# A 1 MB pair transfer issued as two transfers of 512 KB, for even and odd SBUF partitions

## The chip, the cores and the metric

The kernel runs on one core of one Trainium2 chip. Times are microseconds (us) of device time of one execution, as medians of several runs; a profile is one profiled execution, and its span is some 2 us shorter than the run's time.

## The reference, cut to what matters

Each of 65,536 tokens has 1024 numbers, seen as 16 heads of 64. A routing product picks one head per token. That head's 64 numbers are multiplied by that head's 64x64 matrix; all other heads of the output are zero.

```python
# x: (64, 1024, 1024) float32; route_w: (1024, 16); experts: (16, 64, 64)
route_logits = x @ route_w
best_head = np.argmax(route_logits, axis=-1)
x_heads = x.reshape(B, S, H, Dh)
for h in range(H):
    mask = (best_head == h)
    transformed = np.matmul(x_heads[:, :, h, :], experts[h])
    out[:, :, h, :] = transformed * mask[:, :, None]
```

The kernel reads 268 MB and writes 268 MB.

## The kernel before

It works on pairs: 256 tokens, two for each of 128 SBUF partitions, so 8 KB per partition and 1 MB per pair. SyncE (SP) issues every load and store. TensorE (PE) transposes the tokens and multiplies them; the profile counts 108 matmuls for a pair. Five of eight blocks of 128 columns take the "split pass" with small 64x64 matmuls (80 of the 108), three take whole 128x128 blocks (12), and 16 are transposes. The calls of the split pass and of the whole blocks appear as two matmuls each. ScalarE (ACT), VectorE (DVE) and GpSimd (POOL) move results out of PSUM, where this kernel's matmuls put them (the `ps_` tiles), and mask them. SBUF is the memory that holds the tokens; its tiles here have 128 partitions.

```python
P = 128
XIN_BUFS = 10
OUT_BUFS = 6
AHEAD = 7                     # loads run seven pairs ahead
...
xg = x.rearrange("b s d -> (b s) d").rearrange("(g p t) d -> g p t d", p=P, t=2)
og = out.rearrange("b s d -> (b s) d").rearrange("(g p t) d -> g p t d", p=P, t=2)
...
def load(g):
    xin = xin_pool.tile([P, 2, D], FP32, name="xin", tag="xin")
    nc.sync.dma_start(out=xin, in_=xg[g])
    return xin
...
def split_pass(xt):
    ...                       # per token tile: 5 blocks x 4 matmuls of 64x64 on 80 columns
def whole_block(ps, xt, f):
    ...                       # one 128x128 matmul on 144 columns
...
for j in range(-2 * AHEAD, NT + 2, 2):
    if j + 2 * AHEAD < NT:
        xins[j + 2 * AHEAD] = load(j // 2 + AHEAD)
    if j < 0:
        continue
    pair = [i for i in (j - 2, j - 1) if i >= 0]
    for i in pair:
        work[i] = split_pass(xts[i])
    ...                       # transposes of pair j mixed with whole blocks of the pair before
                if i == pair[1]:
                    nc.sync.dma_start(out=og[i // 2], in_=ot)
```

SP works in program order: a store waits for its pair's result (869.7 us in 256 waits for DVE in before), and the next load stands behind it (issued 0.44 us after the store, median of the trace). The build gives DMA transfers eight completion semaphores in turn (both traces show eight for SP), and a transfer waits until the one eight places before it has landed: in after none is issued earlier, and the closest comes 16 ns later. So at most eight transfers of SP are in flight; the traces count at most seven in before.

Of the kernel before, what the change touches and what calls it, by code (L numbers as in the profile page):

```python
# [13 lines left out]
AX = mybir.AxisListType  # L14

P = 128
XIN_BUFS = 10
OUT_BUFS = 6
XT_BUFS = 5
# [5 lines left out]
def kernel(  # L25
# [19 lines left out]
    nc = tc.nc  # L45
# [3 lines left out]
    N = B * S  # L49
    NB = D // P  # L50
    NT = N // P
    HB = 512
# [4 lines left out]
    STEP = 2 * Dh + H  # L57
    assert D % P == 0 and N % P == 0 and Dh * H == D and 2 * Dh == P and NB == 8

    xg = x.rearrange("b s d -> (b s) d").rearrange("(g p t) d -> g p t d", p=P, t=2)  # L60
    og = out.rearrange("b s d -> (b s) d").rearrange("(g p t) d -> g p t d", p=P, t=2)

    consts = ctx.enter_context(tc.tile_pool(name="consts", bufs=1))
    small = ctx.enter_context(tc.tile_pool(name="small", bufs=4))
    xin_pool = ctx.enter_context(tc.tile_pool(name="xin", bufs=XIN_BUFS))
    xt_pool = ctx.enter_context(tc.tile_pool(name="xt", bufs=XT_BUFS))
# [5 lines left out]

    ident = consts.tile([P, P], FP32, name="ident")
    make_identity(nc, ident)
# [8 lines left out]
    with nc.allow_non_contiguous_dma(reason="constants, once"):  # L83
        for ab in range(2):
            e0, r0 = (0, Dh) if ab == 0 else (H, 0)
            for half in range(2):
                nc.scalar.dma_start(  # L87
                    out=mv[half * Dh:(half + 1) * Dh, ab::2, e0:e0 + Dh], in_=ev[half][:, ab:NS:2, :])
            nc.scalar.dma_start(out=mv[:, ab::2, r0:r0 + H], in_=rv[:, ab:NS:2, :])
        for half in range(2):  # L90
            nc.scalar.dma_start(
                out=mf[half * Dh:(half + 1) * Dh, :, H + half * Dh:H + (half + 1) * Dh],
                in_=ev[half][:, NS:, :])
# [7 lines left out]

    def load(g):
        xin = xin_pool.tile([P, 2, D], FP32, name="xin", tag="xin")
        nc.sync.dma_start(out=xin, in_=xg[g])
        return xin

    def transposes(xin, t, xt):

        for half in range(2):
            ps_t = ps_t_pool.tile([P, NB // 2, P], FP32, name="ps_t", tag="ps_t")  # L110
            for q in range(NB // 2):
                p = half * (NB // 2) + q
                nc.tensor.transpose(ps_t[:, q, :], xin[:, t, p * P:(p + 1) * P], ident)  # L113
                if q == NB // 2 - 1:
                    nc.scalar.copy(out=xt[:, half * (NB // 2):(half + 1) * (NB // 2), :], in_=ps_t)  # L115
                yield
# [10 lines left out]
    def split_pass(xt):  # L127
        ps = ps_s_pool.tile([P, 2, HB], FP32, name="ps_s", tag="ps_s")
        for p in range(NS):
            s, ab = divmod(p, 2)  # L130
            o0 = s * STEP + ab * Dh
            for half in range(2):
                for th in range(2):
                    nc.tensor.matmul(  # L134
                        ps[th * 64:(th + 1) * 64, half, o0:o0 + W],
                        lhsT=xt[half * 64:(half + 1) * 64, p, th * 64:(th + 1) * 64],
                        rhs=mv[half * 64:(half + 1) * 64, p, :],
                        start=(p == 0), stop=(p == NS - 1), skip_group_check=True)
        RW = (NS // 2) * STEP + Dh
        raw = raw_pool.tile([P, 2, SLOTS * STEP], FP32, name="raw", tag="raw")  # L140
        nc.scalar.copy(out=raw[:, :, 0:RW], in_=ps[:, :, 0:RW])  # L141
        lgs = small.tile([P, H], FP32, name="lgs", tag="lgs")
        logits(lgs, ps)
        return raw, lgs

    def whole_block(ps, xt, f):
        o0 = f * STEP + Dh
        nc.tensor.matmul(  # L148
            ps[:, o0:o0 + STEP], lhsT=xt[:, NS + f, :], rhs=mf[:, f, :],
            start=(f == 0), stop=(f == NF - 1), skip_group_check=True)  # L150

    def finish(ot, ps, raw, lgs):
        lgw = small.tile([P, H], FP32, name="lgw", tag="lgw")
        logits(lgw, ps)
        lg = small.tile([P, H], FP32, name="lg", tag="lg")
        nc.vector.tensor_add(out=lg, in0=lgs, in1=lgw)  # L156
        mx = small.tile([P, 8], FP32, name="mx", tag="mx")
        nc.vector.max(out=mx, in_=lg)  # L158
        ix = small.tile([P, 8], U32, name="ix", tag="ix")
        nc.vector.max_index(out=ix, in_max=mx, in_values=lg)  # L160
        mask = small.tile([P, H], FP32, name="mask", tag="mask")
        nc.vector.tensor_scalar(  # L162
            out=mask, in0=hid, scalar1=ix[:, 0:1], scalar2=None, op0=ALU.is_equal)

        ov = ot.rearrange("k (p two e) -> k p two e", two=2, e=Dh)
        mk = mask.rearrange("k (p two) -> k p two", two=2)

        def bc(m):
            return m.unsqueeze(3).to_broadcast(list(m.shape) + [Dh])

        nc.vector.tensor_tensor(  # L171
            out=ov[:, NS:], in1=bc(mk[:, NS:]), op=ALU.mult,
            in0=ps[:, W:W + NF * STEP].rearrange("k (f w) -> k f w", w=STEP)[:, :, 0:2 * Dh]
            .rearrange("k f (two e) -> k f two e", two=2))
        rv4 = raw.rearrange("k two (s w) -> k s two w", w=STEP)
        for ab in range(2):
            n = (NS + 1 - ab) // 2
            o0 = ab * W
            nc.gpsimd.tensor_tensor(  # L179
                out=ov[:, ab:NS:2], in0=rv4[:, 0:n, :, o0:o0 + Dh], in1=bc(mk[:, ab:NS:2]),  # L180
                op=ALU.mult)
# [7 lines left out]
# [8 lines that stand above are left out]
        tr = iter(())  # L197
        if j < NT:
            for i in (j, j + 1):
                xts[i] = xt_pool.tile([P, NB, P], FP32, name="xt", tag="xt")  # L200
            xin = xins.pop(j)
            tr = chain(transposes(xin, 0, xts[j]), transposes(xin, 1, xts[j + 1]))
        order = ORDER if pair else "T" * (2 * NB)
        f = 0
        for step in order:
            if step == "T":
                next(tr, None)
                continue
            i = pair[f // NF]
            if f % NF == 0:  # L210
                ps_w = ps_w_pool.tile([P, HB], FP32, name="ps_w", tag="ps_w")
            whole_block(ps_w, xts[i], f % NF)
            f += 1
            if f % NF == 0:
                if i == pair[0]:
                    ot = out_pool.tile([P, 2, D], FP32, name="ot", tag="ot")
                finish(ot[:, i % 2, :], ps_w, *work.pop(i))
                xts.pop(i)
                if i == pair[1]:
                    nc.sync.dma_start(out=og[i // 2], in_=ot)  # L220


# [28 lines left out]
```

## Time and profile before

| | before |
|---|---|
| time, median of 4 runs | 1370.2 us (1369.3 to 1372.3) |
| PE busy | 94% of the span |
| queue q1 (all loads and stores) | 97.6% of 16 engines' time |
| PE waits for "issue" in the split pass | 54.1 us |
| PE waits for a load | 6.5 us |

Lines of the page of before: the span; the busy time and share of the engines; the DMA queues (packets, MB, share of 16 engines' span); the chain of waits by engine; the issues of loads (count, KB each, median us from issue to landing; stores took 12.7 us).

```profile
span 1367.4 us, 65580 instructions
...
PE 1291.7 (94%) x27648; PEld 1210.8 (89%) x27648; DVE 928.0 (68%) x4098; ACT 924.1 (68%) x1537; POOL 721.9 (53%) x1031
...
q1 hardware_dynamic: 73728, 536.90, 97.6%
q8 instruction: 218, 3.57, 1.0%
...
PE 93%; issue 4%; DMA 2%; ACT 0%; DVE 0%; POOL 0%; ACTq 0%; POOLq 0%; DVEq 0%
...
xin<-in_x_dram SPq DMA_DIRECT2D x256, 1024.0 KB, 14.8
...
```

The wait list of PE in before (engine, line, what it waited for: us in total, times, longest in us):

```profile
...
PE ps_s L134 <- issue: 54.1, 71, 2.2
PE ps_t L113 <- DMA xin<-in_x_dram: 6.5, 2, 5.9
...
```

The wait list of SP in before:

```profile
...
SPq L220 <- DVE ot L171: 869.7, 256, 9.0
...
```

Three stretches of before (stretch, length, busy us and count of PE, PE weight loads, DVE, ACT, POOL, then PE clock, DMA share, GB/s):

```profile
...
100.00:300.00 200.00, 191.06 (x4090) 179.04 (x4086) 137.27 (x607) 136.56 (x228) 107.00 (x152) 1.00 1.01 403
300.00:500.00 200.00, 192.79 (x4154) 181.03 (x4144) 139.20 (x612) 138.74 (x231) 108.46 (x155) 1.00 1.01 404
1300.00:1367.40 67.40, 57.73 (x1268) 54.24 (x1260) 44.61 (x198) 41.36 (x69) 35.81 (x52) 0.96 0.73 299
...
```

How to read these. A packet is one piece that one DMA engine moves, here mostly 8 KB: q1 has 65,536 of them in before and 8192 of 4 bytes, 16 for each of the 512 transfers, at 9 ns each (median). The small ones are called completion packets below. PE leads the chain, and it hardly ever waits for data. Its own idle time is "issue", which means that no wait in the profile explains it. The trace does: each such stall ends about 1.4 us after one of the 218 packets of 16 KB on queue q8 has landed; there are 71 waits for 218 packets. q8 carries PE's instructions (27,648 matmuls and as many weight loads in 218 blocks are 254 a block), and PE's stalls stand a multiple of 256 of its instructions apart, give or take one, counted in the trace with the semaphore instructions (55,818 in all, 256 a block; 53 of 67 distances fit exactly, the others miss by one). A fetch takes an engine from q1: while a packet of q8 is in progress, 15.0 packets of q1 are, on average, and otherwise 16.0 (trace, 100 to 1300 us). At the same time the DMA share is 1.01: the engines are never idle in the middle (packet records overlap a little, so a full queue shows slightly over 1). Both resources look full.

The trace's packet records say: an 8 KB packet takes 309 ns in the median and 324.9 ns on average.

### The profile page before, as it was taken

Reading aid. Unit: us, or ns where it says so; the run is one execution under the profiler, and the core shown is the slowest. Engines: PE = TensorE matmul, PEld = TensorE weight load, DVE = VectorE, ACT = ScalarE, POOL = GpSimd, SP = SyncE. Lnnn points to the kernel's source line nnn. Section 1 sums busy time; section 2 is a strip of 40 time slices with the busy share of each in tenths; the row PEclk is TensorE's granted clock in tenths of the full one; section 3 lists DMA queues with packets and bytes.
Section 4 is the critical chain, followed back from the end, with each engine's and each line's share of the span. In section 5 each row is a group of like instructions: output and inputs, shape, how many; then the busy total and the mean of one; then the engine's idle time right before and its main releaser. Section 6 shows DMA issues by size and latency. Waiting matters only on the chain.

```text
span 1367.4 us, 65580 instructions
## 1 busy us (share of the span) xinstructions
PE 1291.7 (94%) x27648; PEld 1210.8 (89%) x27648; DVE 928.0 (68%) x4098; ACT 924.1 (68%) x1537; POOL 721.9 (53%) x1031
## 2 busy tenths in 40 slices
PE   7999999999999999999899999999999998999997
PEld 6899988899889999999899989998899998998996
DVE  3667666667666767667667766766667766766676
ACT  4676666677666667676666666766667666766675
POOL 2555555555555555555555555555555554555555
PEclk9999999999999999999999999999999999999999
DMA  9999999999999999999999999999999999999995
GB/s 348 421 418 407 408 394 400 402 401 409 409 400 397 402 414 411 404 405 402 395 399 397 402 393 406 401 405 393 382 399 409 410 407 388 395 415 393 397 381 220
DMA packets 76214, 541.43 MB, mean 396 GB/s; under 512 B 10384, under 2 KB 10384, under 8 KB 10384
## 3 DMA queue, kind: packets, MB, share of 16 engines
q1 hardware_dynamic: 73728, 536.90, 97.6%
q8 instruction: 218, 3.57, 1.0%
q10 hardware_dynamic: 2192, 0.33, 0.1%
q14 instruction: 76, 0.62, 0.1%
HBM read 268.76 MB, written 268.44 MB: 393 GB/s over the span
## 4 chain that ended last, share of the span: by engine, by line
PE 93%; issue 4%; DMA 2%; ACT 0%; DVE 0%; POOL 0%; ACTq 0%; POOLq 0%; DVEq 0%
PE ps_t L113 35%; PE ps_s L134 30%; PE ps_w L148 27%; DMA xin<-in_x_dram 1%; DMA mv<-in_experts_dram 1%; POOL ot L179 0%; ACT raw L141 0%; ACT L115 0%; ACT xt L115 0%; ACTq L87 0%; POOLq L246 0%; DVE ot L171 0%; DVE ix L160 0%; DVE mask L162 0%; DVE lg L156 0%
## 5 line engine op out<-in xcount | busy, mean ns | idle before, releaser
L179 POOL TENSOR_TENSOR ot<-raw,mask 128x384 f32<-128x384 f32 (+1 forms) x1024 | 721.1, 726 | 640.1 <-ACT xt L115 495.8
L113 PE MATMUL ps_t<-ident,xin 128*128 128x128 f32 x4096 | 756.0, 277 | 11.4 <-DMA xin<-in_x_dram 6.5
L115 ACT COPY xt<-ps_t 128x512 f32<-128x512 f32 x1024 | 576.7, 589 | 278.6 <-PE ps_t L113 278.3
L148 PE MATMUL ps_w<-mf,xt 128*128 128x144 f32 x3072 | 575.4, 287 | 0.4 <-issue 0.4
L113 PEld LDWEIGHTS ps_t<-ident,xin 128*128 128x128 f32 x4096 | 499.5, 141 | 35.5 <-issue 7.4
L134 PE MATMUL ps_s<-mv,xt 64*64 64x80 f32 x20480 | 440.4, 233 | 55.0 <-issue 54.1
L134 PEld LDWEIGHTS ps_s<-mv,xt 64*64 64x64 f32 x20480 | 385.8, 133 | 111.2 <-issue 110.1
L141 ACT COPY raw<-ps_s 128x704 f32<-128x704 f32 x512 | 372.2, 747 | 145.4 <-PE ps_s L134 78.4
L148 PEld LDWEIGHTS ps_w<-mf,xt 128*128 128x128 f32 x3072 | 463.7, 191 | 0.8 <-issue 0.5
L171 DVE TENSOR_TENSOR ot<-ps_w,mask 128x384 f32<-128x384 f32 x512 | 285.6, 558 | 19.0 <-DVE mask L162 0.7
L125 DVE TENSOR_REDUCE lgs<-ps_s 128x16 f32<-128x96 f32 x512 | 129.4, 253 | 197.7 <-ACT raw L141 197.3
L122 DVE TENSOR_REDUCE lgw<-ps_w 128x16 f32<-128x48 f32 x512 | 103.8, 203 | 107.1 <-PE ps_w L148 106.9
L162 DVE TENSOR_SCALAR mask<-hid,ix 128x16 f32<-128x16 f32 x512 | 120.0, 234 | 55.9 <-POOL ot L179 0.9
L156 DVE TENSOR_TENSOR lg<-lgs,lgw 128x16 f32<-128x16 f32 x512 | 111.7, 218 | 17.6
L158 DVE MAX8 mx<-lg 128x8 f32<-128x16 f32 x512 | 91.1, 178 | 17.7
L160 DVE FIND_INDEX8 ix<-mx,lg 128x8 uint32<-128x16 f32 x512 | 86.5, 169 | 0.0
L160 DVE MATCH_VALUE_LOAD ix<-mx,lg 128x8 f32 x512 | 47.2, 92 | 17.7
L115 ACT ACT_TABLE_LOAD x1 | 1.3, 1283 | 9.5 <-DMA mv<-in_experts_dram 9.5
L80 DVE MEMSET mf<- 128x432 f32 x1 | 0.4, 418 | 0.9 <-PEq L235 0.9
masks.py:197 POOL MEMSET ident<- 128x128 f32 x1 | 0.2, 205 | 0.3 <-POOLq L235 0.3
masks.py:199 POOL TENSOR_SCALAR_AFFINE_SELECT ident<-ident 128x128 f32<-128x128 f32 x1 | 0.3, 294 | 0.0
L235 POOL MEMSET const-float32-0.0<- 128x1 f32 x1 | 0.1, 99 | 0.2 <-issue 0.2
(5 smaller groups left out, 0.6 us busy)
## 6 DMA issues: line engine op xcount, KB each, us to landing
xin<-in_x_dram SPq DMA_DIRECT2D x256, 1024.0 KB, 14.8
out_dram<-ot SPq DMA_DIRECT2D x256, 1024.0 KB, 12.7
mv<-in_experts_dram ACTq DMA_DIRECT2D x2, 48.0 KB, 6.4
mf<-in_experts_dram ACTq DMA_DIRECT2D x2, 48.0 KB, 3.9
mv<-in_experts_dram ACTq DMA_DIRECT2D x2, 32.0 KB, 6.4
mv<-in_route_w_dram ACTq DMA_DIRECT2D x1, 24.0 KB, 7.2
mf<-in_route_w_dram ACTq DMA_DIRECT2D x1, 24.0 KB, 2.0
mv<-in_route_w_dram ACTq DMA_DIRECT2D x1, 16.0 KB, 5.7
```

Source lines behind the costliest of these rows:

```text
L113: nc.tensor.transpose(ps_t[:, q, :], xin[:, t, p * P:(p + 1) * P], ident)
L115: nc.scalar.copy(out=xt[:, half * (NB // 2):(half + 1) * (NB // 2), :], in_=ps_t)
L122: nc.vector.tensor_reduce(out=lg, in_=parts.rearrange("k s h -> k h s"), op=ALU.add, axis=AX.X)
L125: nc.vector.tensor_reduce(out=lg, in_=parts.rearrange("k b s h -> k h b s"), op=ALU.add, axis=AX.XY)
L134: nc.tensor.matmul(ps[th * 64:(th + 1) * 64, half, o0:o0 + W], lhsT=xt[half * 64:(half + 1) * 64, p, th * 64:(th + 1) * 64], rhs=mv[half * ...
L141: nc.scalar.copy(out=raw[:, :, 0:RW], in_=ps[:, :, 0:RW])
L148: nc.tensor.matmul(ps[:, o0:o0 + STEP], lhsT=xt[:, NS + f, :], rhs=mf[:, f, :], start=(f == 0), stop=(f == NF - 1), skip_group_check=True)
L156: nc.vector.tensor_add(out=lg, in0=lgs, in1=lgw)
L160: nc.vector.max_index(out=ix, in_max=mx, in_values=lg)
L162: nc.vector.tensor_scalar(out=mask, in0=hid, scalar1=ix[:, 0:1], scalar2=None, op0=ALU.is_equal)
L171: nc.vector.tensor_tensor(out=ov[:, NS:], in1=bc(mk[:, NS:]), op=ALU.mult, in0=ps[:, W:W + NF * STEP].rearrange("k (f w) -> k f w", w=STEP ...
L179: nc.gpsimd.tensor_tensor(out=ov[:, ab:NS:2], in0=rv4[:, 0:n, :, o0:o0 + Dh], in1=bc(mk[:, ab:NS:2]), op=ALU.mult)
```

## The change

The intent: the same bytes in the same 8 KB runs, but in transfers of half the size, so that each one is shorter. Even and odd partitions were chosen so that each half still has rows from end to end of the 128 partitions.

```diff
+WAYS = 2
     def load(g):
         xin = xin_pool.tile([P, 2, D], FP32, name="xin", tag="xin")
-        nc.sync.dma_start(out=xin, in_=xg[g])
+        for r in range(WAYS):
+            nc.sync.dma_start(out=xin[r::WAYS], in_=xg[g, r::WAYS])
         return xin
...
                 if i == pair[1]:
-                    nc.sync.dma_start(out=og[i // 2], in_=ot)
+                    for r in range(WAYS):
+                        nc.sync.dma_start(out=og[i // 2, r::WAYS], in_=ot[r::WAYS])
```

With eight transfers in flight at most, the change also halves the bytes that can be in flight, from 8 MB to 4 MB.

## The prediction

> What bounds the kernel now. Two resources are nearly full. The page gives PE 94% of the span, and the chain of waits is 93% PE. The stretches view gives a DMA share of 1.00 or 1.01 from 20 to 1300 us; queue q1 (all loads and stores) holds 97.6% of 16 engines' time. The trace's packet records: an 8 KB packet takes 309 ns (median; mean 325), 4096 per engine, and each transfer ends with one completion packet of 9 ns per engine. 4096 x 325 ns is 1331 us of the span of 1367.
>
> PE's own idle time is not data. The wait list shows PE waiting for xin only 6.5 us (2 times), but for "issue" 54.1 us in 71 waits at L134. In the trace a pair takes 4.93 us when undisturbed and 5.26 us on average, and each such stall ends about 1.4 us after one of the 218 packets of 16 KB on the instruction queue q8 has landed. So PE waits for its own instructions. [...] A fetch shares the engines with the full q1.
>
> What the change does. The same 65,536 8 KB packets. Issues go from 512 to 1024: SP spends 0.34 us (store) and 0.38 us (load) each, so 1.45 us per pair instead of 0.72; SP otherwise waits (869.7 us for DVE ot), so this is hidden. Completion packets go from 8192 to 16384: 512 more per engine at 6 to 9 ns is 3 to 5 us of DMA time. First and last packets of a transfer run about 10 to 20 ns longer than the middle ones; if that goes with transfers, 512 more boundaries cost about 10 us.
>
> The build rotates eight completion semaphores over SP's transfers, and each transfer waits for the one eight before it. That allowed 8 MB in flight; now 4 MB. Median landing is 14.8 us (loads) and 12.7 us (stores), but eight transfers back is now two pairs, 10.5 us. So SP will wait for landings. [...] Loads land some 20 us before use, so latency itself is off the path.
>
> Gain: smaller transfers may let a PE fetch reach an engine earlier, and shrink the 54 us. But the DMA, at about 99%, then becomes the limit, which leaves at most 1 to 1.5% unless packets also get shorter.
>
> [...]
>
> I predict 1372 us, range 1335 to 1412. Chances: faster by over 2% 0.18, within 2% 0.62, slower by over 2% 0.20.
>
> What would show it right: 16384 completion packets on q1, 512 KB issues, medians to landing of 9 to 11 us; SP's waits name DMA landings; PE busy near 1292 us; DMA share 1.00 in the middle; PE "issue" waits somewhat below 54 us.
>
> What would make it wrong. Faster: fetch waits vanish and mean packet time drops near 313 ns (as from 30 to 100 us, at about 420 GB/s). Slower: [...] (packets well over 309 ns), or the 4 MB window starves engines (DMA share below 0.97), with PE then waiting for xin.

1372 us are 2 us above the measured 1370.2 us; the terms are 3 to 5 us and about 10 us of added DMA time, against a gain of at most 1 to 1.5% (14 to 21 us). With that gain they come to some 1363 to 1372 us, without it to some 1383 to 1385 us.

## More of the kernel before

The experiments ran in three sets (e1 to e4, e5 to e8, e9 to e12), each on another chip and beside runs of the kernel before, whose medians were 1370.8, 1367.4 and 1370.1 us.

In the last 67 us the DMA share is only 0.73, since loads are far ahead: the last one lands at 1332.6 us, 34.8 us before the end, and with only stores left the share is 0.53.

The page's share of q1 times the span gives the engine time that loads and stores took: 0.976 x 1367.4 = 1334.6 us. This number, called q1 time below, is used in all comparisons.

## The result, and the profile after

| | before | after |
|---|---|---|
| time, median of 4 runs | 1370.2 us | 1339.8 us (1336.5 to 1342.5) |
| ratio | | 0.9775 (95% interval 0.975 to 0.980) |
| q1 time | 1334.6 us | 1319.4 us |
| mean 8 KB packet (trace) | 324.9 ns | 319.9 ns |
| packets over 400 ns (trace) | 5.2% | 2.7% |
| time of a pair, mean of pairs 20 to 240 (trace) | 5.27 us | 5.12 us |

A ratio is the mean time of one kernel's fast runs over that of the other's of the same rounds, so it is not quite the ratio of the medians quoted.

The change made the kernel 2.25% faster. Lines of the page of after, as before:

```profile
span 1338.1 us, 66342 instructions
...
PE 1290.3 (96%) x27648; PEld 1208.3 (90%) x27648; DVE 933.7 (70%) x4098; ACT 923.2 (69%) x1537; POOL 721.9 (54%) x1031
...
q1 hardware_dynamic: 81920, 536.94, 98.6%
q8 instruction: 218, 3.57, 1.0%
...
DMA 96%; PE 1%; SPq 0%; DVE 0%; issue 0%; POOL 0%; ACT 0%; ACTq 0%; POOLq 0%; DVEq 0%
...
xin<-in_x_dram SPq DMA_DIRECT2D x512, 512.0 KB, 10.2
...
```

From the list of all waits in after:

```profile
...
PE ps_s L136 <- issue: 21.9, 35, 1.8
...
DVE ot L173 <- DMA out_dram<-ot: 83.8, 104, 1.8
...
POOL ot L181 <- DMA out_dram<-ot: 76.3, 40, 3.0
...
```

The wait list of SP in after:

```profile
...
SPq L223 <- DMA out_dram<-ot: 373.2, 469, 1.7
SPq L106 <- DMA xin<-in_x_dram: 335.6, 496, 2.0
...
```

The same kind of stretches in after:

```profile
...
100.00:300.00 200.00, 194.13 (x4142) 181.73 (x4144) 139.25 (x617) 138.30 (x232) 107.75 (x153) 1.00 1.01 410
300.00:500.00 200.00, 197.10 (x4298) 185.82 (x4291) 143.16 (x632) 142.88 (x238) 111.97 (x160) 1.00 1.00 404
1300.00:1338.00 38.00, 23.57 (x524) 21.58 (x518) 20.78 (x88) 16.39 (x28) 16.89 (x24) 0.85 0.81 333
...
```

What to see. PE's busy time is unchanged (1291.7 and 1290.3 us), but its issue waits fell from 54.1 to 21.9 us. The chain turned over: it was PE 93%, it is DMA 96%. SP now spends 373.2 + 335.6 us waiting for landings, and in the later part DVE and POOL wait for free output buffers (83.8 and 76.3 us, against 0.7 us for DVE before).

The order in time is instructive. In the stretch from 100 to 500 us the wait list gives PE 16.0 us of issue waits before and 7.8 us after. PE got through more matmuls there (4142 + 4298 against 4090 + 4154), faster than the loads could follow: in the trace, the time between issuing a load and PE's first use of it is 34 to 37 us at every twentieth pair before, but falls from 32 us (pair 20) over 23 us (pair 100) to 14 us (pair 160) after, and stays there. From then on the DMA sets the pace.

So the span's 29.3 us can be split by the page, one profile of each kernel. All queues together filled 98.8% of 1367.4 us = 1351.0 us before and 99.8% of 1338.1 us = 1335.4 us after: 15.6 us are DMA work that became shorter, though 8192 completion packets were added. The other 13.7 us are DMA idle time that vanished. Most of that is the end: from 1300 us on, idle time was (1 - 0.73) x 67.4 = 18.2 us and is (1 - 0.81) x 38.0 = 7.2 us, because loads no longer finish so far ahead of PE: the last one lands 24.6 us before the end, and 34.8 us in before.

Two things need a cause: why PE's fetch waits shrank, and why the same 8 KB packets take less time.

### The profile page after: what moved, and what is told of

It is laid out like the page before. It is cut to its first block, busy times and chain, and to the rows that moved or that the text cites. A ratio compares the mean times of both kernels' runs of the same rounds, so it can differ in the third digit from the quotient of the medians.

```text
span 1338.1 us, 66342 instructions
## 1 busy us (share of the span) xinstructions
PE 1290.3 (96%) x27648; PEld 1208.3 (90%) x27648; DVE 933.7 (70%) x4098; ACT 923.2 (69%) x1537; POOL 721.9 (54%) x1031
## 4 chain that ended last, share of the span: by engine, by line
DMA 96%; PE 1%; SPq 0%; DVE 0%; issue 0%; POOL 0%; ACT 0%; ACTq 0%; POOLq 0%; DVEq 0%
DMA out_dram<-ot 95%; DMA xin<-in_x_dram 1%; SPq L106 0%; PE ps_w L150 0%; PE ps_t L115 0%; DMA mv<-in_route_w_dram 0%; PE ps_s L136 0%; POOL ot L181 0%; DVE ot L173 0%; ACTq L88 0%; ACT raw L143 0%; ACT xt L117 0%; DVE mask L164 0%; POOLq L249 0%; DVE lg L158 0%
## 5 line engine op out<-in xcount | busy, mean ns | idle before, releaser
L136 PE MATMUL ps_s<-mv,xt 64*64 64x80 f32 x20480 | 430.0, 232 | 22.6 <-issue 21.9
L136 PEld LDWEIGHTS ps_s<-mv,xt 64*64 64x64 f32 x20480 | 381.1, 133 | 73.2 <-issue 62.8
L173 DVE TENSOR_TENSOR ot<-ps_w,mask 128x384 f32<-128x384 f32 x512 | 285.6, 558 | 98.5 <-DMA out_dram<-ot 83.8
L127 DVE TENSOR_REDUCE lgs<-ps_s 128x16 f32<-128x96 f32 x512 | 121.4, 251 | 106.3 <-ACT raw L143 105.4
L158 DVE TENSOR_TENSOR lg<-lgs,lgw 128x16 f32<-128x16 f32 x512 | 131.8, 257 | 17.6
## 6 DMA issues: line engine op xcount, KB each, us to landing
xin<-in_x_dram SPq DMA_DIRECT2D x512, 512.0 KB, 10.2
out_dram<-ot SPq DMA_DIRECT2D x512, 512.0 KB, 10.2
```

The costliest lines, as they stand in the source:

```text
L127: nc.vector.tensor_reduce(out=lg, in_=parts.rearrange("k b s h -> k h b s"), op=ALU.add, axis=AX.XY)
L136: nc.tensor.matmul(ps[th * 64:(th + 1) * 64, half, o0:o0 + W], lhsT=xt[half * 64:(half + 1) * 64, p, th * 64:(th + 1) * 64], rhs=mv[half * ...
L158: nc.vector.tensor_add(out=lg, in0=lgs, in1=lgw)
L173: nc.vector.tensor_tensor(out=ov[:, NS:], in1=bc(mk[:, NS:]), op=ALU.mult, in0=ps[:, W:W + NF * STEP].rearrange("k (f w) -> k f w", w=STEP ...
```

## The experiments

Theory A: it is the smaller amount in flight. Theory B: it is the smaller size of a transfer, which disturbs PE's instruction fetches less and is disturbed less by them. A third idea came from the trace of before: 1216 packets of 570 to 600 ns, most of them some 2 to 4 us after SP issues a store and a load 0.44 us apart; after has only 155 of them.

### Whole transfers with 4 MB in flight (e1_window4)

Each transfer additionally waits for the landing of the fourth before it. Size unchanged.

```diff
+    def bounded(inst):
+        if len(sent) >= 4:
+            tc.add_manual_dep(inst.ins, sent[-4].ins.name, ... Sync, DATA ...)
+        sent.append(inst)
-        nc.sync.dma_start(out=xin, in_=xg[g])
+        bounded(nc.sync.dma_start(out=xin, in_=xg[g]))
                                          # the store likewise
```

> Whole 1 MB transfers as before, but each waits until the fourth transfer before it has landed, so at most 4 MB are in flight, as with the halves. Theory A (the gain comes from the smaller amount in flight, which is a side effect of eight completion semaphores used in turn): 1335 to 1348 us, PE waits for issue at the L134 matmuls near 22 us, share of long packets (over 400 ns) near 0.03. Theory B (the gain comes from the smaller size of a transfer): 1362 to 1380 us, issue waits near 54 us, long packets near 0.05.

Measured: 1359.7 us (1351.9 to 1370.1), ratio 0.9937 (0.9867 to 1.0006). The profiled run was the fastest, so its lines flatter the variant. From its page:

```profile
span 1350.1 us, 65585 instructions
...
q1 hardware_dynamic: 73728, 536.90, 98.0%
...
```

And from its list of all waits:

```profile
...
PE ps_s L144 <- issue: 36.7, 56, 1.5
...
```

Landings came down to 10.2 us, exactly as in after, but the time did not follow: it fell between the two ranges that I had named. Only 136 packets of 570 to 600 ns are left, and even so the time barely moves. With the same 4 MB in flight, halves are about 20 us faster. Theory A alone doesn't hold, but this run doesn't clear it of a part. The interval allows a gain of 1.3%, and in the profiled run, the fastest, q1 time was 0.980 x 1350.1 = 1323.1 us: 11.5 of the 15.2 us that after saves came with whole transfers too. The copies below (e9) and the halves with less in flight (e12) test theory A again.

### The transfers alone: 1 MB and 512 KB (e2_dma_only_1mb, e3_dma_only_512k)

All compute is removed; each pair is stored from the tile it was loaded into. The result is wrong on purpose.

```diff
-    ... transposes, matmuls, masks ...
+    for g in range(NT // 2 + AHEAD):
+        if g < NT // 2:
+            xins[g] = load(g)
+        if g >= AHEAD:
+            nc.sync.dma_start(out=og[g - AHEAD], in_=xins.pop(g - AHEAD))   # e3: two halves
```

> Wrong result on purpose: no compute, each loaded pair is stored again from its own tile, whole 1 MB transfers in the same order. It measures what the DMA alone needs. If the DMA was the limit before (my prediction): 1330 to 1350 us. If PE's instruction waits were the limit and packets are long only because of what PE's fetches and the bursts do: 1275 to 1310 us, mean 8 KB packet near 312 ns.

> As the run without compute, with the halves for even and odd partitions. If halves cost DMA time by their completion packets only: 3 to 6 us more than with 1 MB. If halves make packets shorter by themselves: 15 us or more less.

Measured: 1269.4 us (1269.2 to 1269.6) with 1 MB and 1274.3 us (1274.2 to 1274.4) with halves. From the page of the copy with 1 MB:

```profile
...
q1 hardware_dynamic: 73728, 536.90, 100.4%
...
HBM read 268.76 MB, written 268.44 MB: 424 GB/s over the span
...
```

And of the copy with halves:

```profile
...
q1 hardware_dynamic: 81920, 536.94, 100.4%
...
```

This was the step that broke my model: the copy came out below both ranges. Nearly every packet takes 309 ns here, and the copy needs 1269 us, not the 1331 us that I had taken as the DMA's fixed demand. It runs at 424 GB/s over the span. So in the full kernel about 1334.6 - 1272.9 = 61.7 us of q1 time is lengthening that something else on the core causes. "Lengthening" means the time that packets take beyond what the same packets take when nothing else runs. And halves by themselves are no help: they cost 4.9 us, as predicted (512 more completion packets for each engine, 9.0 ns each in the trace, are 4.6 us).

### Quarters (e4_quarters)

```diff
-WAYS = 2
+WAYS = 4
```

> Four transfers of 256 KB for every fourth partition, 2 MB in flight at most. If smaller transfers, or less in flight, help further: 1310 to 1335 us with issue waits under 15 us. If 2 MB is too little to keep 16 engines fed, or SP's issues (about 0.36 us each, 2.9 us per pair) get in the way: over 1345 us with a DMA share under 0.97.

Measured: 1581.4 us (1580.9 to 1585.6), ratio 1.154. A piece of the instruction timeline of SP in this run (start us, us, engine, line, operation):

```profile
...
600.30 2.66 SPq L223 DMA_DIRECT2D out_dram<-ot  x4
603.06 3.65 SPq L106 DMA_DIRECT2D xin<-in_x_dram  x4
...
```

SP is the new limit, as far as the profile shows. Four stores and four loads, issued without a break, take 2.66 + 3.65 us here, and a pair takes 6.1 us (trace, mean of pairs 20 to 240). One issue takes 0.59 us in the median, against 0.34 and 0.38 us for stores and loads before and 0.50 us after. It isn't only the number of issues: a load of all 128 partitions takes 0.33 us where it stands alone (SP's timeline in e5) and 0.38 us within 0.2 us of the store before it (before), while halves take 0.50 us although 1006 of the 1024 issues start over 0.2 us after the one before (after). In its whole wait list SP has some 130 us of waits in 1579 us, where after it had over 800. Packets got longer as well: the page gives q1 93.5%, so 1476.5 us of q1 time, and the mean 8 KB packet is 356 ns in the trace. Why was not tested, so it isn't separated what each of the two costs. Smaller is not simply better.

### Spreading the issues (e5_spread_issues)

Whole transfers; a load waits for the first matmul of the split pass, and the store is issued after it in program order.

```diff
+        inst = nc.sync.dma_start(out=xin, in_=xg[g])
+        tc.add_manual_dep(inst.ins, <first split-pass matmul>, ... Sync, DATA ...)
...
-                    nc.sync.dma_start(out=og[i // 2], in_=ot)
+                    held = (i // 2, ot)      # issued after the next load
```

> Whole 1 MB transfers and no limit on bytes in flight, but the load of a pair is issued about 2 us after the store before it and about 3 us before the next one, not 0.4 us after the store: it waits for the first matmul of the split pass. In the trace of before some 1250 packets take 570 to 600 ns and fall 2.0 to 3.7 us after the pair of issues; with 4 MB in flight or with halves nearly all are gone. If the issue of store and load in one burst makes them: under 200 such packets, mean packet 320 ns, 1350 to 1362 us. If not: over 800 such packets and 1366 to 1376 us.

Measured: 1365.6 us (1357.1 to 1366.9), ratio 0.9967 (0.9918 to 1.0016), between the two ranges that I had named. The 570 to 600 ns packets did go, from 1216 to 80, so they go with the burst of issues, and q1 time fell to 0.973 x 1363.5 = 1326.7 us. But no gain in time is shown: the chain is PE's as before, so 8 us of shorter packets are probably worth little here. The medians to landing fell too, to 9.3 and 9.1 us.

### The copy with PE beside it (e6_copy_pe_1mb, e7_copy_pe_512k, e8_copy_pe_few)

The copy again, and beside it only PE, on constants, waiting for no data. In e6 and e7 it runs the kernel's 108 matmuls a pair in the same three forms; in e8 only 6 calls of 512 columns a pair, which the profile shows as 12 matmuls, so PE is busy all the time with few instructions. One run each. Their outputs are wrong, which doesn't matter for the times.

```diff
+    def pe_pair():
+        ...      # e6, e7: the calls of a pair's split passes, transposes and whole blocks, on constants
+        ...      # e8: for k in range(6): matmul of 128x128 weights on 512 columns
         if g >= AHEAD:
             nc.sync.dma_start(out=og[g - AHEAD], in_=xins.pop(g - AHEAD))   # e7: two halves
+            pe_pair()
```

> Wrong result on purpose: the DMA copy without compute (1269 us) and beside it only PE, which runs the kernel's 27,648 matmuls of the same three forms on constants and waits for no data. If PE's instruction fetches cost the DMA only their own 218 packets: 1280 to 1290 us, packets near 310 ns. If fetches are what makes packets long: over 1310 us, mean packet over 318 ns. If fetches queue behind 1 MB transfers, PE shows issue waits of 50 us or more here too.

> As the copy with PE's matmuls, with halves. If the size of a transfer decides how long a fetch waits: issue waits at most half of those with 1 MB, and PE's last matmul earlier. If the amount queued on an engine decides, also less, since 4 MB are in flight and not 8; then the run with whole transfers and 4 MB in flight (issue waits 36.7 us against 54.1) tells the two apart.

> Wrong result on purpose: the copy with 1 MB transfers and PE busy with 6 matmuls of 512 columns a pair, so PE reads SBUF all the time but needs only about 13 instruction fetches and not 218. If PE's reading of SBUF makes packets long: mean packet over 315 ns. If fetches do: 309 to 310 ns and 1270 to 1275 us.

Measured: 1335.6 us, 1316.4 us and 1325.3 us. Lines from the page of the copy with PE and 1 MB transfers:

```profile
span 1333.8 us, 56122 instructions
...
q1 hardware_dynamic: 73728, 536.90, 98.8%
q8 instruction: 216, 3.54, 0.9%
...
```

Its wait list of PE:

```profile
...
PE ps_s L201 <- issue: 25.7, 52, 1.2
...
```

The page of the copy with PE and halves:

```profile
span 1314.6 us, 56388 instructions
...
q1 hardware_dynamic: 81920, 536.94, 98.9%
...
```

Its wait list of PE:

```profile
...
PE ps_s L203 <- issue: 18.8, 45, 0.9
...
```

And the page of the copy with few PE instructions:

```profile
span 1323.5 us, 6967 instructions
...
PE 1320.2 (100%) x3072; PEld 584.2 (44%) x3072; DVE 1.4 (0%) x3; POOL 0.8 (0%) x7
...
q1 hardware_dynamic: 73728, 536.90, 96.2%
...
q8 instruction: 24, 0.39, 0.1%
...
```

The last run is the control. PE is busy for all of it, and the q1 time is 0.962 x 1323.5 = 1273.2 us, the same as with no PE at all (its span is PE's; the copy was through some 54 us earlier). So a busy PE that reads SBUF, at least with such wide matmuls and fewer weight loads, does not lengthen packets. (It needed 24 fetches, 256 of its 6144 matmuls and weight loads each. I had expected 13, having counted a call as one matmul: 3072 instructions are some 12 blocks of 254, as in before.) With the kernel's matmuls, and so 216 blocks of instructions, q1 time rises to 0.988 x 1333.8 = 1317.8 us. The lengthening, 44.9 us, goes with the instruction stream, and the only DMA traffic that differs is the fetches themselves. They are 3.54 MB, under 1% of the bytes: 216 packets of about 0.93 us are some 12.6 us for each of 16 engines on their own queue, and the 44.9 us come on top. One forecast failed: if fetches queued behind 1 MB transfers, I expected 50 us or more of issue waits here too, and there are 25.7.

The trace of these runs shows more than the sums. Here is what the DMA moved in 40 equal slices of the span, first in the copy with PE and 1 MB transfers:

```profile
...
GB/s 341 423 423 423 422 415 411 416 415 413 418 408 418 411 413 412 408 391 417 413 415 397 387 422 416 423 420 412 418 413 408 389 419 414 416 414 415 359 354 294
...
```

And in the copy with few PE instructions:

```profile
...
GB/s 344 427 426 428 427 427 427 427 427 427 427 427 427 428 427 427 426 426 428 427 428 427 427 427 427 427 427 426 427 427 428 427 427 427 427 427 427 427 105 0
...
```

From 30 to 130 us PE runs its full stream in e6 (97.9 us busy, 16 fetches), and yet packets take 311.3 ns on average. From 1200 to 1300 us PE is as busy (98.1 us, 17 fetches), and they take 343.5 ns. So the lengthening is neither a fixed price of a fetch nor one of PE's reading of SBUF: it builds up and varies. In e8, where fetches are far apart, some 23 packets over 400 ns start 0.5 to 1 us after one of the 24 fetches, and nothing more follows.

With halves q1 time is 0.989 x 1314.6 = 1300.1 us. Against the copy with halves alone (1277.7 us) the lengthening is 22.4 us: about half. This is one run against one, and the stretch from 1200 to 1300 us in e6 alone holds 9.8 us of lengthening (1.4 us in e7), so the size of the gain is rough. PE's issue waits fall from 25.7 to 18.8 us, so not by half in this setting. That speaks for theory B without the other engines of the real kernel; but halves have 4 MB in flight here too, which the next run tests.

### The copy with PE, 1 MB transfers and 4 MB in flight (e9_copy_pe_window4)

The edit is the wait of e1_window4 in e6_copy_pe_1mb.

> Wrong result on purpose: the copy with whole 1 MB transfers and PE's matmuls beside it (1335.6 us with 8 MB in flight), now with 4 MB in flight, as the copy with halves has (1316.4 us). If the amount in flight makes the packets shorter: 1314 to 1322 us, mean packet near 315 ns. If the size of a transfer does: 1330 to 1340 us, near 320 ns. In between: both.

Measured: 1352.5 us (1348.9 to 1359.3). From the page of this run:

```profile
span 1348.9 us, 55881 instructions
...
q1 hardware_dynamic: 73728, 536.90, 98.1%
...
```

Its wait list of PE:

```profile
...
PE ps_s L211 <- issue: 42.0, 71, 1.5
...
```

None of the outcomes that I had named came; it is above both other times. With whole transfers, fewer in flight made matters worse than the single run with 8 MB (1335.6 us). So in the copy less in flight is not what helps. With equal bytes in flight halves win by 36 us (1352.5 against 1316.4), and with an equal number of transfers in flight by 19 us (1335.6 against 1316.4). The q1 time says the same, without PE's part in the end of the span: 0.981 x 1348.9 = 1323.3 us here, 1317.8 us with 8 MB in flight, 1300.1 us with halves. Keep in mind that the other two are single runs on another chip, and that the four runs here spread over 10 us.

### Only the stores as halves (e10_stores_only)

```diff
-        for r in range(WAYS):
-            nc.sync.dma_start(out=xin[r::WAYS], in_=xg[g, r::WAYS])
+        nc.sync.dma_start(out=xin, in_=xg[g])
```

> Only the stores are issued as halves, loads stay whole: one part of the change alone, 768 transfers, eight of them hold about 5.3 MB. If the gain grows with the number of places where a fetch may get in and with less in flight: 1350 to 1360 us, PE issue waits of 30 to 45 us. If it needs both: 1365 to 1373.

Measured: 1369.5 us (1365.5 to 1379.0), ratio 0.9970 (0.9892 to 1.0049). From the list of PE's waits in the profiled run, the slowest:

```profile
...
PE ps_s L135 <- issue: 55.5, 74, 2.0
...
```

Half of the change gives nothing that can be told from zero (the interval allows a gain of 1.1%); PE's fetch waits are as in before. Halved stores alone don't do it. Whether halved loads alone would do was not run.

### Contiguous halves (e11_contiguous_halves)

```diff
-            nc.sync.dma_start(out=xin[r::WAYS], in_=xg[g, r::WAYS])
+            lo, hi = r * P // WAYS, (r + 1) * P // WAYS        # written out in the kernel
+            nc.sync.dma_start(out=xin[lo:hi], in_=xg[g, lo:hi])
                                          # the store likewise
```

> Halves of 512 KB as after, but partitions 0 to 63 and 64 to 127 and not even and odd ones. If it does not matter which partitions make a half: 1335 to 1345 us. If [...]: packets well over 309 ns (median over 450) and over 1600 us.

The second case is the one in which it does matter which partitions make a half. Its figures are a forecast that no earlier run supports.

Measured: 1745.5 us, one run. From its page:

```profile
span 1743.7 us, 66342 instructions
...
q1 hardware_dynamic: 81920, 536.94, 98.2%
...
```

In the trace 40% of the packets take over 400 ns (2.7% after), with a mean of 415 ns (319.9 after). The median is still 313 ns, so I was too pessimistic about the median and right about the direction. Why these packets are longer was not shown. That even and odd partitions are used is not a detail: with contiguous halves the same size and number of transfers make the kernel much slower (1745.5 against 1339.8 us).

### Halves with at most six in flight (e12_halves_window6)

The kernel after, with the wait of e1_window4 at a distance of six.

> The kernel after with at most six halves (3 MB) in flight and not eight. If less in flight keeps packets shorter, as whole transfers with 4 MB suggest: 1325 to 1335 us, mean packet under 318 ns. If 3 MB is too little to cover a landing and the next issue: 1342 us or more, DMA share under 0.99.

Measured: 1339.9 us (1337.7 to 1341.8), ratio 0.9763 against before. From its page:

```profile
...
q1 hardware_dynamic: 81920, 536.94, 98.5%
...
xin<-in_x_dram SPq DMA_DIRECT2D x512, 512.0 KB, 7.6
...
```

Landings came down to 7.6 us, the time and the q1 time (0.985 x 1338.0 = 1317.9 us) stayed; neither outcome that I had named came. It is the same as after, and this is what one expects if the amount in flight plays no part. No version that beats the kernel after was found.

## Why the prediction was right or wrong

The time lay inside the range (1335 to 1412), near its fast end: the forecast of 1372 us was 32 us off, and it was the width of the range that covered it. The most likely class, "within 2%", was wrong: I gave faster by over 2% only 0.18, and it was 2.25%.

- "PE waits for its own instructions": right. It was the term that moved. Issue waits fell from 54.1 to 21.9 us. My "somewhat below 54" was too timid.
- "But the DMA, at about 99%, then becomes the limit, which leaves at most 1 to 1.5% unless packets also get shorter": this is the step that was mis-sized. The DMA did become the limit (chain 96% DMA). But I took 1331 us as fixed demand. The copy alone needs 1273 us of q1 time; about 62 us were lengthening, and 45 us of lengthening appear as soon as PE's instruction stream runs beside a copy. Halves cut that lengthening to 22 us in the copy, and the kernel's q1 time by 15.2 us. The rest of the gain, the 13.7 us of DMA idle time that vanished, is 1.0% and so within the 1 to 1.5%.
- What I left out: the loads' lead is a store of time. PE ahead of the DMA shortened the lead from some 35 us to 14 us, and that took 11 us of DMA idle time off the end of the span (18.2 against 7.2 us from 1300 us on).
- "512 more per engine at 6 to 9 ns is 3 to 5 us of DMA time": right, 4.9 us in the copy.
- "512 more boundaries cost about 10 us": wrong. In the copy packets stay at 309 ns with either size; the longer first and last packets of before do not come from boundaries as such.
- "SP will wait for landings", "medians to landing of 9 to 11 us": right (10.2 us, and 708.8 us of waits). The starving of engines didn't happen: the DMA share stayed at 1.00 to 1.01.
- "packets well over 309 ns": not so with even and odd partitions (mean 319.9 ns, median 309 ns). With contiguous halves the mean is 415 ns.

What stays open. How a smaller transfer reduces the lengthening is argued, not shown. A fetch perhaps gets in between transfers or parts of them. The trace fits that loosely: a fetch started about 3.3 us (median) after PE entered a block in the kernel before, about the same with 4 MB in flight and whole transfers, and 2.9 us after; the places of the blocks are inferred here from where the stalls fall. Nor is it known how the lengthening builds up, or which part of PE's stream starts it: e6 and e8 differ in the fetches, but also in the form of the matmuls and the number of weight loads. The size of a transfer and the rows in it (every second partition) changed together, and the one run that kept the size and changed the rows (e11) made packets much longer (415 ns) for a reason that was not shown, so the order of rows is a rival that stands untested. It isn't known why halved stores alone do nothing. And of the 61.7 us of lengthening in before, the copy with PE explains 44.9 us; what makes the rest, beyond the burst of issues, was not separated.

## What to carry to other kernels

A DMA share of 1.00 says that the engines are busy, not that the work can't shrink (q1 time was 1334.6 us here, and 1272.9 us in the copy): run the copy alone to find its floor before you call the DMA the limit. In this kernel, with 55,296 matmuls and weight loads, 218 instruction fetches shared the DMA engines with the data (1.0% of their time), and smaller transfers cut PE's "issue" waits from 54.1 to 21.9 us. So when such waits stand on PE's chain, try smaller transfers; make them of even and odd partitions, not of upper and lower ones (1339.8 against 1745.5 us here), and stop before SP's issues become the limit (0.59 us each with quarters, and 1581.4 us). Look at packet times over the run and not only at their mean, since lengthening can build up while the load on PE stays the same (311.3 to 343.5 ns in e6). Test a side effect such as "less in flight" by itself, since here it looked like the cause and by itself gave 1.3% at most.
